# Splitting one product of three blocks into seven inner products, in a pooling mixer kernel with float32 accuracy

## The chip, the cores and the metric

The kernel runs on one core of a Trainium2 chip. The metric is the device time of one execution in microseconds (us). Engines are named as the profile names them: PE is TensorE (matmuls), PEld its weight loads, DVE is VectorE, ACT is ScalarE, POOL is GpSimd, SP is SyncE, which here issues DMAs.

## The reference

Of the hybrid trunk only the pooling layer runs, since the depth is 1. With x of 4096 rows and 1024 columns, all in float32:

```python
normed = rms_norm(h, norm_w[i])                 # row-wise, 1024 columns
u, gate = jnp.split(normed @ in_w, 2, axis=-1)  # in_w: 1024 x 2048
ug = u.reshape(b, s, 4, 256)
pooled = stack(trailing_mean(ug[:, :, g], w) for g, w in enumerate((2, 4, 8, 16))) - ug
mixed = jnp.einsum('bsgc,gcd->bsgd', pooled, group_w) + group_b
y = mixed.reshape(b, s, 1024) * scale * jax.nn.silu(gate)
h = h + y @ out_w                               # out_w: 1024 x 1024
out = rms_norm(h, final_norm_w)
```

Nearly all the arithmetic is in two matrix products, `normed @ in_w` and `y @ out_w`.

## The kernel before, in words

**Exactness.** Every float32 operand is held as a pair of tiles: a rounded copy (`copy`, L165, on ACT) and the rest (`sub`, L159, on DVE). `split` makes the pair. One product of two such operands is three matmuls (`mm3`, L603): high by high, high by low, low by high.

**Seven products in place of eight.** Each large product is one level of the Strassen-Winograd scheme: P1 to P7, where sums and differences of quarter matrices are formed on DVE beforehand and results are accumulated in PSUM banks. A step is one of these products. There are 28 steps of the first input phase ("a": half of the input projection, four blocks of 1024 rows), 28 of the second ("b": the other half, same rows, normalized operands read back from DRAM), and 56 of the output phase ("o", eight blocks of 512 rows).

**A step of phase b** (`product_in`) multiplies two operand tiles of 128 x 1024 pairs (`t[0]`, `t[1]`) by weight tiles `w[i]`. Weights of 128 x 128 are loaded and 512 columns stream by, 48 matmuls in all. The order of steps is P1, P2, P7, P6, P5, P4, P3. P1, P2, P7 and P4 use banks 0 to 3 ("x" and "v"), P6, P5 and P3 banks 4 to 7 ("y"). P1 goes bank by bank and its sums are copied to the y banks as seeds; the others go through `t[0]` for all four banks, then `t[1]`. After each step `evict_in` copies or adds the banks into SBUF: after P2 four ACT copies with Silu, after P7 four ACT copies to `ev["22"]`, after P5 and P4 DVE additions.

**Buffers.** Four operand tiles `ops` (op0 to op3) are used in turn, two by a step, so the pair for the next step is made while the present one multiplies. Eleven tiles `st` and eight wider tiles `vt` hold everything else: raw operands loaded ahead, evicted results, weights being prepared, window sums. `take` hands out the one that has been free longest, `give` returns it. Who waits for whom through these tiles is decided by this order.

**The order of work.** The program is written step by step; a scheduler places the instructions on each engine's queue, and each engine then takes its queue in that order. In each turn of the step loop: loads for up to three steps ahead are issued (`load`), the operand pair for the next step is made (`split_step`), sums for the step after that are formed (`form`), window sums that have come due are computed (`pool`: scans L755, L801, L806, then a store to `yd`), the step itself runs (`run`). In blocks 1 and 2 of phase b the weights of the output phase are prepared after P5 (`make_wo`: four loads of `out_w`, scaled on ACT at L246, combined on DVE, stored to `wod`). In block 3 each step is followed by `load_w`: the output phase's weights for the same product are loaded from `wod` and split into the same `w` tile that the step has just used. DMAs of these kinds all go through SP's queue.

**Where the same scheme is already used.** In the output phase from block 2 on, P2 is split into seven inner products (`product_inner`, L701), with 256 columns in each matmul.

Of the kernel before, what the change touches and what calls it, by code (L numbers as in the profile page):

```python
# [10 lines left out]
F32 = mybir.dt.float32  # L11
# [4 lines left out]
P = 128  # L16
D = 1024
# [47 lines left out]
def kernel(  # L65
# [59 lines left out]
    st.renew = renew  # L125
    vt = Slots(
        [mem.tile([P, 2 * (HIST + H)], F32, tag=f"vt{i}", name=f"vt{i}") for i in range(NV)]
    )
# [368 lines left out]


    xs = [{} for _ in range(NB)]
    turn = [0]  # L500
# [6 lines left out]
    first_saves = []  # L507

    def split_halves(us, saved=None):
        ts = []  # L510
        for h, u in enumerate(us):
            t = next_op("p (s a b) -> p s a b", s=2, a=2)
            split(t, u)
# [33 lines left out]
    def form_in(q, b, i):  # L547

        s = xs[b]
        if i in (P1, P2):  # L550
            if q == 0:
                for u in s["11" if i == P1 else "12"]:
                    normalize(b, 0, u)
        elif i == P7:
            if q == 0:
                for h in range(2):
                    normalize(b, 1, s["21"][h])
                    sub(s["21"][h], s["11"][h], s["21"][h])
        elif i == P6:
            s["2"] = [take(pool=early if (q, b) == (0, 0) else None) for _ in range(2)]  # L560
            for h in range(2):
                if q == 0:
                    normalize(b, 1, s["22"][h])
                sub(s["2"][h], s["22"][h], s["21"][h])
            for u in s.pop("21"):
                give(u)
            if q == 0:
                give(rstd.pop(b))
        elif i == P5:
            for h in range(2):  # L570
                add(s["11"][h], s["2"][h], s["11"][h])
            if (q, b) != (0, 0):
                for u in s.pop("2"):
                    give(u)

    def split_in(q, b, i):
        s = xs[b]
        key = {P1: "11", P2: "12", P6: "2", P7: "21", P5: "11", P4: "22", P3: "12"}[i]
# [11 lines left out]
    stores = []  # L590

    def form_s4(b):
        for u, s2 in zip(xs[b]["12"], xs[b]["2"]):
# [49 lines left out]
    def form_inner(stage):  # L643

        pattern, sizes = "p (n k s a) -> p n k s a", dict(n=2, k=2, s=2)
        if stage == 0:
            us = inner_w.pop("raw")
            b11, b12 = (quarter(us[0], j) for j in range(2))
            b21, b22 = (quarter(us[1], j) for j in range(2))
            raw = inner_w["sums"] = [take(pattern, **sizes) for _ in range(2)]  # L650
            (t3, t2), (t1, t4) = ([r[:, n] for n in range(2)] for r in raw)
            sub(t3, b22, b12)
            add(t2, t3, b11)
            sub(t1, b22, t2)
# [5 lines left out]
        hi, lo = (kept.pop().rearrange(pattern, **sizes) for _ in range(2))  # L660
# [483 lines left out]
    def run(n, between=None, behind=None, seeds=4):  # L1144
# [3 lines left out]
            product_out(i, split_up.pop(n), sets, n == len(steps) - 1)  # L1148
            evict_o(b, i, sets)
        else:  # L1150
            product_in(i, split_up.pop(n), sets, i == P1, between, behind)
            evict_in(b, 0 if kind == "a" else 1, i, sets, seeds)

    pending = []

# [204 lines left out]

    scales, summed = {}, []
    stages = (P6, P5, P4)
    stages = (P6, P5, P4)

    for n in range(2, len(steps)):
        kind, b, i = steps[n]
# [121 lines left out]
```

## Time and profile before

| what | value |
|---|---|
| median of 3 runs | 910.34 us (910.04 to 911.31) |
| the profiled execution | 910.49 us, span 908.7 us |
| PE busy | 900.7 us, 99% of the span, 4320 matmuls |
| DVE busy | 715.5 us, 79% |
| ACT busy | 485.9 us, 53% |
| chain that ended last | PE 95% of it |

The span is the time between the first and the last instruction; the execution's own time has 1.8 us around it. A group row reads: line, engine, operation, output<-input, shapes, count, then busy time in all and the mean of one in ns, then idle time of the engine just before them and what ended it. A timeline row reads: start and length in us, engine, line, operation, and in brackets the idle time before it with its releaser. A windows row has the busy time of each engine in one stretch, then the granted PE clock and the share of the DMA engines.

### The profile page before, as it was taken

The page shows a single profiled execution, that of the slowest core. Times are in us where ns is not written, and L with a number is a line of the kernel's source. Part 1 is how long each engine was busy: PE and PEld are TensorE (multiplying, and loading weights), DVE is VectorE, ACT ScalarE, POOL GpSimd, SP SyncE. Part 2 cuts the span into 40 slices and gives each one's busy share as a digit, 9 for nine tenths or more (in the row PEclk, how much of TensorE's full clock was granted, in tenths as well). Part 3 has the DMA queues.
Part 4 walks back from the last instruction along what each step waited for, and adds up shares of the span by engine and source line. Part 5 has one row for each costly group of instructions (what it writes and reads, how often), then busy time and mean ns, then how long its engine had stood idle before and what let it go on. Part 6 is the DMA issues. An engine that isn't in the chain of part 4 may idle for free.

```text
span 908.7 us, 11590 instructions
## 1 busy us (share of the span) xinstructions
PE 900.7 (99%) x4320; PEld 790.1 (87%) x4320; DVE 715.5 (79%) x843; ACT 485.9 (53%) x735; POOL 84.6 (9%) x166
## 2 busy tenths in 40 slices
PE   9999999999999999999999999999999999999997
PEld 7888888888888888888888888888888898988886
DVE  3889995985995997685786599599759768868686
ACT  7869547447446555355345445645545535445444
POOL 0020100100110000000000000001122113212200
PEclk9999999999999999999999999999999999999999
DMA  9987776577575454134616715618585675675732
GB/s 343 401 300 230 268 241 240 190 267 245 218 271 193 162 207 140 47 140 138 255 72 217 267 70 174 200 54 225 179 234 160 169 205 162 163 220 156 180 139 94
DMA packets 70841, 178.10 MB, mean 196 GB/s; under 512 B 6528, under 2 KB 24320, under 8 KB 70784
## 3 DMA queue, kind: packets, MB, share of 16 engines
q1 hardware_dynamic: 58160, 144.82, 46.0%
q0 software_dynamic: 11904, 31.48, 13.3%
q10 hardware_dynamic: 720, 1.06, 0.3%
q8 instruction: 34, 0.56, 0.3%
q14 instruction: 23, 0.19, 0.1%
HBM read 116.50 MB, written 60.83 MB: 195 GB/s over the span
## 4 chain that ended last, share of the span: by engine, by line
PE 95%; DVE 2%; DMA 1%; ACT 1%; issue 0%; DVEq 0%; ACTq 0%; SPq 0%
PE bank L603 89%; PE bank L701 3%; PE bank L406 3%; DMA st<-wvd 1%; DMA t3d<-st 0%; DMA early<-in_group_w 0%; DVE vt L1067 0%; DVE st L159 0%; ACT st L974 0%; ACT st L446 0%; DVE vt L162 0%; PE bank L472 0%; DVE op L159 0%; DVE vt L1026 0%; DVE st L156 0%
## 5 line engine op out<-in xcount | busy, mean ns | idle before, releaser
L603 PE MATMUL bank<-op,w 128*128 128x512 f32 x2688 | 581.2, 379 | 0.2 <-ACT st L165 0.2
L603 PEld LDWEIGHTS bank<-op,w 128*128 128x128 f32 x2688 | 507.8, 189 | 72.9 <-ACT st L165 0.6
L603 PE MATMUL bank<-w,op 128*128 128x512 f32 (+1 forms) x1212 | 262.2, 377 | 0.0
L603 PEld LDWEIGHTS bank<-w,op 128*128 128x128 f32 x1212 | 226.0, 189 | 31.0
L159 DVE TENSOR_TENSOR op<-st,op 128x1024 fp32r<-128x1024 f32 x129 | 156.5, 1220 | 76.4 <-ACT op L165 76.0
L165 ACT ACTIVATE op<-st 128x1024 fp32r<-128x1024 f32 x129 | 134.7, 1052 | 123.3 <-PE bank L603 82.6
L165 ACT ACTIVATE vt<-bank 128x512 f32<-128x512 f32 x105 | 61.4, 593 | 44.7 <-PE bank L603 44.2
L159 DVE TENSOR_TENSOR op<-vt,op 128x1024 fp32r<-128x1024 f32 x43 | 52.4, 1220 | 20.8 <-ACT op L165 20.6
L165 ACT ACTIVATE op<-vt 128x1024 fp32r<-128x1024 f32 x43 | 45.0, 1052 | 28.9 <-PE bank L603 24.9
L165 ACT ACTIVATE st<-bank 128x512 f32<-128x512 f32 x67 | 39.0, 592 | 38.0 <-PE bank L603 26.1
L884 POOL DMA_DIRECT2D st<-in_x x19 | 16.9, 894 | 387.7 <-DVE op L159 354.1
L159 DVE TENSOR_TENSOR st<-st,st 128x1024 f32<-128x1024 f32 (+1 forms) x43 | 46.7, 1108 | 3.2 <-ACT st L943 1.3
L165 ACT ACTIVATE bank<-bank 128x512 f32<-128x512 f32 x48 | 27.9, 581 | 35.6 <-PE bank L603 35.4
L755 DVE TENSOR_TENSOR_SCAN vt<-vt,window 128x1040 f32<-128x1040 f32 x16 | 38.1, 2379 | 2.8 <-ACT vt L165 2.7
L159 DVE TENSOR_TENSOR w<-st,w 128x1024 fp32r<-128x1024 f32 x25 | 30.2, 1220 | 11.7 <-ACT w L165 11.7
L165 ACT ACTIVATE w<-st 128x1024 fp32r<-128x1024 f32 x25 | 26.0, 1052 | 16.3 <-PE bank L603 10.8
L806 DVE SCALAR_TENSOR_TENSOR st<-vt,colt,st 128x512 f32<-128x512 f32 x46 | 32.4, 746 | 1.7 <-ACT st L165 1.6
L165 ACT ACTIVATE st<-st 128x1024 f32<-128x1024 f32 x16 | 16.9, 1058 | 29.9 <-DVE st L156 29.7
L801 DVE SCALAR_TENSOR_TENSOR vt<-vt,vt 128x1024 f32<-128x1024 f32 x24 | 29.3, 1221 | 0.3
L947 DVE SCALAR_TENSOR_TENSOR vt<-vt,ors,st 128x1024 f32<-128x1024 f32 x18 | 22.5, 1282 | 8.0 <-POOL ors L225 8.0
L162 DVE TENSOR_TENSOR st<-st,vt 128x1024 f32<-128x1024 f32 x22 | 26.1, 1216 | 2.1 <-DMA vt<-rd 2.1
L1067 DVE TENSOR_TENSOR st<-bank,st 128x512 f32<-128x512 f32 x23 | 15.8, 689 | 13.8 <-PE bank L603 13.7
(136 smaller groups left out, 661.6 us busy)
## 6 DMA issues: line engine op xcount, KB each, us to landing
st<-in_xt SPq DMA_DIRECT2D x28, 512.0 KB, 5.9
sd<-st POOLq DMA_DIRECT2D x28, 512.0 KB, 4.3
st<-sd SPq DMA_DIRECT2D x24, 512.0 KB, 4.4
yd<-st SPq DMA_DIRECT2D x23, 512.0 KB, 2.6
st<-in_x SPq DMA_DIRECT2D x20, 512.0 KB, 6.3
st<-yd SPq DMA_DIRECT2D x20, 512.0 KB, 4.7
out<-vt SPq DMA_DIRECT2D x18, 512.0 KB, 4.5
st<-wod SPq DMA_DIRECT2D x15, 512.0 KB, 3.4
```

The lines of the kernel that those rows point to most:

```text
L159: return nc.vector.tensor_tensor(out=dst, in0=a, in1=b, op=ALU.subtract)
L162: nc.vector.tensor_tensor(out=dst, in0=a, in1=b, op=ALU.mult)
L165: return nc.scalar.activation(dst, src, func)
L406: latest[0] = nc.tensor.matmul(ps, a[:, kk, 2 * j + t, :], maps, start=t + m == 0, stop=t == 1 and m == len(pairs) - 1,).ins
L603: latest[0] = nc.tensor.matmul(ps, a, b, start=start and n == 0, stop=stop and n == 2, skip_group_check=True).ins
L701: latest[0] = nc.tensor.matmul(ps, x1, x2, start=i in (P1, P7) and k + n == 0, stop=k == 1 and n == 2, skip_group_check=True,).ins
L755: nc.vector.tensor_tensor_scan(out=sums_[:, HIST:], data0=flat[:, HIST:], data1=flat[:, HIST - win : 2 * end - win], initial=first_sum, op ...
L801: nc.vector.scalar_tensor_tensor(out=s[:, :, at : at + H], in0=s[:, :, at : at + H], scalar=1.0 / win, in1=v[:, :, HIST:], op0=ALU.mult, o ...
L806: nc.vector.scalar_tensor_tensor(out=sg[:, j], in0=s[:, j, at : at + H], scalar=bias_c[2 * grp + j], in1=sg[:, j], op0=ALU.add, op1=ALU.mult,)
L884: nc.gpsimd.dma_start(out=hs[b][half, j][:, n], in_=x[row_of(b, half, j), n * H : (n + 1) * H], accum_op=ALU.add,)
L947: nc.vector.scalar_tensor_tensor(out=us[j], in0=us[j], scalar=rs[:, j : j + 1], in1=fw[0], op0=ALU.mult, op1=ALU.mult,)
L1067: partial["added"] = nc.vector.tensor_tensor(out=dst, in0=src, in1=dst, op=ALU.add).ins
```

## The change

In blocks 1, 2 and 3 of phase b, the step P7 is itself computed by seven inner products of half the size in each direction (p1 to p7 below, to tell them from the outer ones). Block 0 is left as it is.

Each inner product multiplies a 256 x 256 part of the weights into one of four "cells" of the banks (two half banks each; cell 0 and 2 in banks 0 and 1, cell 1 and 3 in banks 2 and 3), in 12 matmuls of 256 columns. No further bank is used: p5 goes to cell 3 and is copied out to an SBUF tile `held`, p1 to cell 1, and running sums are moved from cell to cell by ACT copies (`move`). At the end two DVE additions put `held` back into banks 2 and 3.

P7's operands now fill all four `ops` tiles: `front` (for p5, p3) and the first raw operand (p1) are made while P2 runs, `back` (p7, p6) when P2's first half has let its tile go (`second`), the second raw operand (p2, p4) after P2's evictions (`third`). The pair for the next step, P6, is no longer made one step ahead: it is made inside P7, its first half after p2 and its second after p4 has been written down (`middle`, `end`), in the tiles that p1 and p6/p7 let go. The list `ops` is rotated to the order in which they come free.

The weights of the inner products are formed once, in steps P6, P5, P4 and P3 of block 0 (`form_seven`): t3 is loaded again from `t3d`, four differences are formed, one pair goes into the quarter of `w[P7]` that is no longer needed, three pairs into `st` tiles that stay taken until block 3's P7 is over.

```diff
     def renew(t):
         i = next(i for i, u in enumerate(sts) if u is t)
-        return mem.tile([P, D], F32R, tag=f"st{i}", name=f"inner{i}")
+        return mem.tile([P, 2, H], F32R, tag=f"st{i}", name=f"inner{i}")
...
     def next_op(pattern, **sizes):
-        t = ops[turn[0] % 4]
-        turn[0] += 1
+        t = ops.pop(0)
+        ops.append(t)
         return t.rearrange(pattern, **sizes)
...
+    def inner_in(q, b, i):
+
+        return q == 1 and b > 0 and i == P7
...
+    def split_seven(s):
+
+        us = s["21"]
...
+        front, back = (take("p (n k s a) -> p n k s a", n=2, k=2, s=2) for _ in range(2))
+        sub(back[:, 0], a11, a21)
+        sub(back[:, 1], a22, back[:, 0])
+        add(front[:, 0], back[:, 1], a11)
+        sub(front[:, 1], a12, back[:, 1])
...
+        sums(front, (P5, P3))
+        plain_op(0, {P1: 0})
+
+        def second():
+            sums(back, (P7, P6))
+
+        def third():
+            plain_op(1, {P2: 0, P4: 1})
+            for u in s.pop("21"):
+                give(u)
+            ops[:] = [ops[n] for n in (1, 2, 0, 3)]
...
+    def form_seven(stage):
+
+        if stage == 0:
+            seven["raw"] = [take() for _ in range(2)]
+            for h, u in enumerate(seven["raw"]):
+                nc.sync.dma_start(out=u, in_=t3d[h])
+            return
...
+    def product_seven(t, v, middle, end):
+
+        def cell(n, c):
+            return v[2 * (n % 2) + c][:, n // 2 * 256 : (n // 2 + 1) * 256]
+
+        def into(i, n):
+            for c in range(2):
+                cs = slice(c * P, (c + 1) * P)
+                for k in range(2):
+                    a = [o[:, k, cs] for o in seven_w[i]]
+                    b = [o[k] for o in t[i]]
+                    for m, (x1, x2) in enumerate(((a[0], b[0]), (a[0], b[1]), (a[1], b[0]))):
+                        latest[0] = nc.tensor.matmul(
+                            cell(n, c).rearrange("p (a s) -> p a s", s=2), x1, x2,
+                            start=i == P5 and k + m == 0, stop=k == 1 and m == 2,
+                            skip_group_check=True,
+                        ).ins
+
+        def move(dst, src):
+            for c in range(2):
+                copy(cell(dst, c), cell(src, c))
+
+        held = take()
+        into(P5, 3)
+        into(P1, 1)
+        for c in range(2):
+            copy(held[:, c, 0:256], cell(3, c))
+        move(0, 1)
+        into(P6, 1)
+        into(P2, 0)
+        move(2, 1)
+        middle()
+        into(P7, 2)
+        into(P3, 1)
+        move(3, 2)
+        into(P4, 2)
+        end()
+        for c in range(2):
+            bank = v[2 + c].rearrange("p (j b) -> p j b", j=2)
+            add(bank, bank, held[:, c, 0:256].unsqueeze(1).to_broadcast([P, 2, 256]))
+        give(held)
...
+            q = 0 if kind == "a" else 1
+            if inner_in(q, b, i):
+                us, parts = xs[b]["2"], []
+                at["split"] += 1
+
+                def next_half():
+                    parts.append(split_half(us[len(parts)]))
+
+                product_seven(split_up.pop(n), sets["v"], next_half, next_half)
+                if b == NB - 1:
+                    give_kept(*places_in)
+                split_up[n + 1] = parts
+            else:
+                product_in(i, split_up.pop(n), sets, i == P1, between, behind)
+            if "second" in seven:
+                seven.pop("second")()
+            evict_in(b, q, i, sets, seeds)
+            if "third" in seven:
+                seven.pop("third")()
+            if inner_in(q, b, i):
+                form_s4(b)
+                for u in xs[b].pop("2"):
+                    give(u)
...
     def split_reach(kind, b, i):
+        if kind == "b" and b > 0 and i == P6:
+            return 0
         return 2 if kind == "o" and (b, i) != (0, P1) else 1
...
+        if kind == "b" and b == 0 and i in forming_seven:
+            with tc.issue_after(latest_split[0]), tc.issue_after(latest_copy[0]):
+                form_seven(forming_seven.index(i))
```

More of the change, by code (lines that the diff above doesn't have):

```diff
@@ L122, in renew, with give_kept, next_kept @@
         i = next(i for i, u in enumerate(sts) if u is t)
-        return mem.tile([P, D], F32R, tag=f"st{i}", name=f"inner{i}")
+        return mem.tile([P, 2, H], F32R, tag=f"st{i}", name=f"inner{i}")
     st.renew = renew
+    def give_kept(*places):
+        for i in places:
+            sts[i] = mem.tile([P, D], F32, tag=f"st{i}", name=f"st{i}")
+            Slots.clock += 1
+            st.free.append((Slots.clock, sts[i]))
+    def next_kept():
+        return next(i for i, u in enumerate(sts) if u is st.free[0][1])
     vt = Slots(
@@ new lines @@
+    seven_w, kept_in, places_in = {}, [], []
+    def form_seven(stage):
[4 more added lines that the diff above has]
+            return
+        us = seven["raw"]
+        if stage == 1:
+            t1, t3 = (us[0][:, :, j * 256 : (j + 1) * 256] for j in range(2))
+            t4, t2 = (us[1][:, :, j * 256 : (j + 1) * 256] for j in range(2))
+            sub(t1, t3, t1)
+            sub(t3, t2, t3)
+            sub(t2, t2, t1)
+            sub(t4, t4, t2)
+            seven["sums"] = {P5: t1, P6: t2, P7: t3, P4: t4}
+            for p, (h, j) in {P1: (0, 0), P2: (1, 0), P3: (1, 1)}.items():
+                seven_w[p] = [w[P7][h][:, v, :, j * 256 : (j + 1) * 256] for v in range(2)]
+            for _ in range(3):
+                places_in.append(next_kept())
+                kept_in.append(st.keep())
+            return
+        for p in ((P5, P6), (P7, P4))[stage - 2]:
+            if p == P5:
+                home = [w[P7][0][:, v, :, 256:512] for v in range(2)]
+            else:
+                t = kept_in.pop().rearrange("p v (k c) -> p v k c", k=2)
+                home = [t[:, v] for v in range(2)]
+            latest_copy[0] = copy(home[0], seven["sums"][p]).ins
+            latest_split[0] = sub(home[1], seven["sums"][p], home[0].bitcast(F32)).ins
+            seven_w[p] = home
+        if stage == 3:
+            for u in seven.pop("raw"):
+                give(u)
@@ L659, in form_inner @@
         r = inner_w["sums"][stage - 1]
[L660 removed]
+        hi, lo = (
+            kept.pop().rearrange("p x (y s a) -> p x y s a", y=2, s=2) for _ in range(2)
+        )
         copy(hi, r)
```

44 lines of the change are left out of this document (35 added, 9 removed).

## The prediction

> **What bounds the kernel now.** First the page's busy times, then PE's own waits, then windows cut at step boundaries:
>
> ```profile
> span 908.7 us, 11590 instructions
> PE 900.7 (99%) x4320; PEld 790.1 (87%) x4320; DVE 715.5 (79%) x843; ACT 485.9 (53%) x735; POOL 84.6 (9%) x166
> ...
> PE bank L603 <- ACT st L165: 0.2, 1, 0.2
> ...
> 397.30:469.80 72.50, 72.50 (x338) 63.48 (x337) 53.15 (x53) 34.66 (x52) 0.00 (x0) 1.00 0.46 167
> 542.30:552.70 10.40, 10.40 (x50) 9.11 (x49) 9.67 (x12) 5.22 (x10) 0.00 (x0) 1.00 0.29 110
> 552.70:563.00 10.30, 10.30 (x50) 9.01 (x49) 10.11 (x9) 5.68 (x9) 0.00 (x0) 1.00 0.66 218
> 563.00:573.40 10.40, 10.40 (x50) 9.11 (x49) 8.13 (x7) 7.16 (x10) 0.00 (x0) 1.00 0.40 115
> ```
>
> PE is the bound: in the large products it waited 0.2 us in all. Block 1 takes 72.50 us for seven steps, so 10.36 each. Whatever shortens PE's work shortens the run, and every new PE wait lengthens it. The last three rows are P1, P2 and P7 of block 3: DVE is busy 9.67, 10.11 and 8.13 of some 10.3 us there, so around this P7 DVE has almost nothing free.
>
> **The gain.** From the chain of waits and the groups:
>
> ```profile
> 702.93 3.35 PE bank L701 x30
> 706.28 2.59 PE bank L603 x12
> ...
> L603 PE MATMUL bank<-op,w 128*128 128x512 f32 x2688 | 581.2, 379 | 0.2 <-ACT st L165 0.2
> L701 PE MATMUL bank<-inner,op 128*128 128x256 f32 x144 | 20.0, 275 | 0.0
> L701 PEld LDWEIGHTS bank<-inner,op 128*128 128x128 f32 x144 | 18.9, 191 | 0.7
> ```
>
> A 256-column matmul costs 3.35/30 = 0.112 us, a 512-column one 2.59/12 = 0.216. P7 goes from 48 x 0.216 = 10.36 to 84 x 0.112 = 9.38: 0.98 us a block, 2.94 in three. This is the whole gain.
>
> The Trainium skill (TensorE: Matmul & The Clock Gate, Part 3, "What overlaps and what doesn't") has it that a weight load overlaps running matmuls only where they use other rows of the array. By that each of the 84 would add its own load, and the change would lose far more than it saves. The row of 30 in 3.35 us, each with a 128x128 load, does not bear it out.
>
> **Hand-offs inside P7** (blocks 1 to 3). Sizes:
>
> ```profile
> 418.07 0.60 ACT L165 ACTIVATE vt<-bank 128x512 f32<-128x512 f32 x1 [0.70 <-PE bank L603]
> 418.56 1.99 ACT L165 ACTIVATE op<-st 128x1024 fp32r<-128x1024 f32 x2
> ...
> L974 ACT ACTIVATE st<-vt 128x512 f32<-128x512 f32 x5 | 3.2, 633 | 9.1 <-DVE vt L711 7.0 <-DVE vt L1067 2.0
> L974 ACT ACTIVATE st<-vt 128x256 f32<-128x256 f32 x2 | 0.8, 409 | 0.0
> ...
> 220.27 0.61 ACT st L165
> 220.88 0.04 issue
> 220.92 482.01 PE bank L603 x2232
> ...
> 220.92 0.92 PE L603 MATMUL bank<-op,w 128*128 128x512 f32 x3 [0.22 <-ACT st L165]
> ```
>
> 418.07 is P2's fourth eviction in block 1. Its last matmul runs 0.38, the next enters after 0.22, and the copy follows the drain by 0.04, so P7 entered at 417.87. A copy thus starts 0.20 us after its bank's last matmul has been followed. The next ACT instruction enters 0.49 later. A 256-column copy is 0.60 - (0.633 - 0.409) = 0.37 long and holds ACT 0.27. PE resumes 0.04 after a copy, and the three matmuls then take 0.92 where 2 x 0.216 + 0.38 = 0.81 is normal: 0.15 in all.
>
> With t from P7's start and 0.67 for six matmuls (one column of an inner product): p5's second column waits for the fourth eviction, 0.20 + 0.60 + 0.15 = 0.95 against 0.67: lost 0.28. p1 ends at 2.96. Only when its first column is done (2.29, seen at 2.49) can ACT copy p5 to `held` (0.27) and p1 to cell 0 (0.37): 3.13, p6 at 3.28: lost 0.32. p2 runs to 5.97, the move that p7 needs ends at 5.87, p7 at 6.02: lost 0.05. p7 and p3 run to 8.70, but on ACT the split of P6's second half (1.0 us, behind p7's end at 7.56) stands before the next move: that one ends at 8.88, p4 at 9.03: lost 0.33. Sum 0.98: P7 takes 10.36 again, +0.0 a block. Bounds from these rows: every hand-off covered, -0.98; twice the losses, +1.0. I take the walk. The two DVE additions at the end are free, under P6 in the other banks.
>
> **Formation of weights, block 0**: two 512 KB loads on SP, four ACT copies of 0.6, eight DVE instructions of 0.68 (5.4 us). Cover is the rest of DVE's queue in P6 to P3, and window sums slide by as much. By the queues of the changed kernel the first casualty would be a seed copy of block 1's P1 standing on ACT behind a "tails" copy that waits for a scan; it comes out level with PE. 0 taken, at most 1.0.
>
> **Block 2.** Added there and in block 3: two splits (ACT 1.0, DVE 1.2 each), four sums (0.62 each), and two tiles from `take`, beside three `st` tiles that stay taken.
>
> ```profile
> 465.77 1.23 DVE L159 TENSOR_TENSOR op<-st,op 128x1024 fp32r<-128x1024 f32 x1 [0.79 <-ACT op L165]
> 412.71 1.34 ACT L246 ACTIVATE st<-st,colt 128x512 f32<-128x512 f32 x2 [3.46 <-DMA st<-in_out_w]
> ...
> L755 DVE TENSOR_TENSOR_SCAN vt<-vt,window 128x1040 f32<-128x1040 f32 x16 | 38.1, 2379 | 2.8 <-ACT vt L165 2.7
> L806 DVE SCALAR_TENSOR_TENSOR st<-vt,colt,st 128x512 f32<-128x512 f32 x46 | 32.4, 746 | 1.7 <-ACT st L165 1.6
> ...
> L156 DVE TENSOR_TENSOR st<-bank,st 128x512 f32<-128x512 f32 x32 | 20.8, 682 | 0.0
> ...
> st<-in_out_w SPq DMA_DIRECT2D x6, 512.0 KB, 4.0
> st<-wod SPq DMA_DIRECT2D x15, 512.0 KB, 3.4
> ...
> yd<-vt SPq DMA_DIRECT2D x9, 512.0 KB, 3.5
> ```
>
> A load of `out_w` goes into the tile of P7's raw operand, behind the subtraction that reads it last. Its scaling (two on ACT, 1.24 us) stands in ACT's queue before the evictions of P2's banks 1 to 3. From the split of P2's first operand (465.77 before, 468.0 when one scan with its follow-up has slid behind, 3.5 us into a stretch with some idle time) to the end of that subtraction DVE has two scans (2.38), four sums (0.62 pitch), four L806 (0.67 pitch), seven full-size ones (1.14 pitch) and 0.3 of small ones, 18.2 us: 486.2. Load 3.4 to 3.5 (the low end of such loads, whose median here is 4.0), scaling 489.8 to 491.0, banks 1 and 2 to 492.1, PE at 492.3; P7 is due at 490.4. Lost 1.9 in place of 0.28, so +1.6 for the block. Bounds: with 465.77 as start only the 0.28 (+0.0); with a load of 4.5, +2.7.
>
> **Block 3.**
>
> ```profile
> 540.43 2.38 DVE L755 TENSOR_TENSOR_SCAN vt<-vt,window 128x1040 f32<-128x1040 f32 x1 [0.91 <-ACT vt L165]
> 546.58 2.38 DVE L755 TENSOR_TENSOR_SCAN vt<-vt,window 128x1040 f32<-128x1040 f32 x1
> 552.33 1.23 DVE L159 TENSOR_TENSOR w<-st,w 128x1024 fp32r<-128x1024 f32 x1 [0.66 <-ACT w L165]
> 553.47 1.22 DVE L159 TENSOR_TENSOR op<-st,op 128x1024 fp32r<-128x1024 f32 x1
> ...
> 551.24 1.06 ACT L165 ACTIVATE w<-st 128x1024 fp32r<-128x1024 f32 x1 [0.50 <-PE bank L603]
> 559.43 1.06 ACT L165 ACTIVATE w<-st 128x1024 fp32r<-128x1024 f32 x1 [3.79 <-DMA st<-wod]
> 560.40 1.07 ACT L165 ACTIVATE vt<-bank 128x512 f32<-128x512 f32 x2
> 561.81 0.60 ACT L165 ACTIVATE st<-bank 128x512 f32<-128x512 f32 x1 [0.35 <-PE bank L603]
> ```
>
> Before, the two scans of block 2's last group run under P1 (540, 546). In the changed queues the first one writes the tile that held `front`, free only when `front` is split at P1's end, so DVE idles under P1 and the scans follow after 552.33. From there its queue is, by 1.14 pitch: w1 552.33, front 553.47, scan 554.7, w1 557.0, first raw operand, two subtractions (the first frees the tile that w2's load needs: 560.5), L801, `back` 562.7, two L806 to 565.3, scan to 567.6, w2, L801, second raw operand 569.8 to 571.0.
>
> ACT's queue: w2 (load 560.6 + 3.4 = 564.0), evictions of banks 0 and 1 (these write tiles that the two L806 read), second raw operand, two small copies behind the second scan (567.6), and only then the evictions of banks 2 and 3, which p5 needs. The tile of the first is on its way to `yd` until 565.35 + 3.5 = 568.85. So p5 enters at 568.87 + 0.60 + 0.15 = 569.6 where 562.9 was due: lost 6.7. p5 and p1 end at 572.3. Behind the first copy to `held` stands the second half of w2 on ACT: its load follows DVE's 571.0, lands at 574.45; split (0.95), `held`, move: PE resumes p6 at 576.2, lost another 3.9. Then 0.05, and 0.4 before p4. Sum 11.1 - 0.98 = **+10.1**. Before, the third eviction ended at 562.4, and PE needed that bank only 2.6 us into P7: cover of 3 us. Bounds: if only one of the two long waits is met, +6; if loads take 4.5 each and the store as well, +12.5.
>
> In the other queues: w7, w6 and later loads slip on SP behind the same two tiles, but the output phase needs them from 615 us on.
>
> **Sum.** 0.0 (block 0) + 0.0 + 1.6 + 10.1 = +11.7 on the profiled execution's 910.49 (span 908.7; the median of the runs, 910.34, is 0.15 below): **922.2 us**. Own range 916.5 (+6 in block 3 alone) to 926.7 (+1.0, +2.7 and +12.5).
>
> **Rivals.**
> - *Faster.* DVE and ACT reach P2's third eviction in time in block 3 (the second scan over by 559) and most hand-offs are covered: -2.94 + 1 = 908.5. For it: DVE is 79% busy over the run. Against: 10.11 of 10.3 us in P2 of block 3.
> - *No change.* The queues keep up, the hand-offs cost what the columns save: 910.6. For it: +0.0 in block 1.
> - *Weight loads not covered.* 0.19 us each on top of 0.112: 84 x 0.30 = 25 us in place of 10.36, three times: 955. Against: the L701 rows.
> - *The clock drops in the 6.7 us gap.* The rows below: PE's last matmul ends at 902.1, and a mean clock of 0.83 over the last 3.7 us is half speed from about 907.4, 5.3 us later. Half speed for p5 and p1 hides under w2's load; if it lasts some 5.6 us beyond, +2.8: 925. The Trainium skill (TensorE: Matmul & The Clock Gate, Part 1, "What's actually happening") gives an idle window of about 3.4 us; the trace's end agrees that a gap of this size is enough.
> - *Knock-on.* Later steps of block 3 or the first output blocks wait for operands too: 928 and up. Against: by the queues, nothing PE needs is late once P7 is over.
>
> ```profile
> 898.82 3.27 PE L603 MATMUL bank<-w,op 128*128 128x512 f32 x26
> 905.00:908.70 3.70, 0.00 (x0) 0.00 (x0) 0.32 (x1) 0.15 (x1) 0.00 (x0) 0.83 0.44 166
> ```
>
> **Chances.** Forecast 0.62, clock 0.10, knock-on 0.08, no change 0.09, faster 0.08, weight loads 0.03. A difference of 0.2% (1.8 us) is about what a measurement of this kernel can tell. Faster 0.08, same 0.09, slower 0.83. Range 912.5 to 928.5: from where slower begins, through the forecast's own range, to the clock case on top of its middle and the mildest knock-on. It leaves out faster, unchanged and the weight loads.
>
> **What would show it.** Right: PE waits of some 6 and 4 us in block 3's P7, released by ACT copies of the line of `copy`; scans of the last group after P1 instead of under it; 0.3 us waits before p5's second column, p6 and p4 in block 1; 256-column matmuls at 0.112. Wrong: block 3's evictions of banks 2 and 3 near 562; PE waits under 1 us there; or new waits outside P7.

## The result, and the profile after

The changed kernel takes 924.21 us (median; 923.57 to 925.47), the kernel before 910.19 us in the same comparison (909.97 to 911.31): ratio 1.0153, 95% interval 1.0136 to 1.0171. The forecast was 922.2 us. The profiled execution has a span of 922.9 us against 908.7. The page, then PE's own waits in the large products:

```profile
span 922.9 us, 11895 instructions
PE 904.6 (98%) x4428; PEld 795.6 (86%) x4428; DVE 736.1 (80%) x875; ACT 498.6 (54%) x769; POOL 85.1 (9%) x166
...
PE bank L708 <- ACT vt L175: 7.4, 2, 5.5
PE bank L708 <- ACT bank L175: 2.0, 1, 2.0
```

Where PE waited 0.2 us before, it now waits 9.4 us, in three places, all at matmuls of the new product (L708) and all released by ACT copies (L175). To see where the 14.2 us arose I compare the start of the same matmul in both traces, counted through the records (36 more in each of three blocks, e4's filling matmuls left out), and take the increase from one step boundary to the next. The same table serves the experiments. All values are us:

| stretch | after | e1 | e2 | e3 | e4 | e5 | e6 | e7 | e8 | e9 | e10 |
|---|---|---|---|---|---|---|---|---|---|---|---|
| start to block 1 | -0.16 | -0.95 | 0.02 | 0.82 | -0.40 | -0.55 | -0.50 | 1.60 | -0.24 | 1.75 | 0.64 |
| block 1: P1, P2 | 0.30 | 0.80 | 0.25 | 0.00 | 0.00 | 0.10 | 0.08 | 0.00 | 0.34 | 0.00 | 0.61 |
| block 1: P7 | 0.11 | 0.00 | 0.12 | 0.12 | 0.12 | 0.11 | 0.12 | -0.41 | -0.41 | -0.39 | -0.55 |
| block 2: to P7's entry | 2.15 | 2.07 | 2.25 | 2.12 | 2.20 | 0.00 | 2.20 | 0.00 | 0.00 | 0.00 | 0.00 |
| block 2: P7 | -0.07 | 0.00 | -0.07 | 1.35 | -0.07 | 0.11 | -0.07 | 1.68 | -0.40 | -0.39 | -0.55 |
| block 3: P1, P2 | 0.00 | 0.00 | 1.27 | 0.00 | 0.00 | 0.00 | 1.44 | 0.00 | 0.00 | 0.00 | 0.00 |
| block 3: P7's entry | 5.62 | 0.25 | 2.89 | 5.62 | 5.62 | 5.61 | 0.00 | 2.69 | 0.00 | 0.00 | 0.00 |
| block 3: P7 | 5.58 | 2.63 | 1.45 | 1.67 | 0.01 | 5.55 | 0.16 | 3.40 | 0.61 | -0.39 | -0.44 |
| rest of block 3, output phase | 0.28 | 4.30 | 0.25 | 0.26 | 0.27 | 0.34 | 0.26 | 0.25 | 0.25 | 0.25 | 0.32 |
| tail | 0.34 | 0.36 | 0.35 | 0.33 | 0.34 | 0.34 | 0.33 | 0.34 | 0.34 | 0.34 | 0.35 |
| span | 922.9 | 918.2 | 917.5 | 921.0 | 916.8 | 920.3 | 912.7 | 918.3 | 909.2 | 909.9 | 909.1 |

Block 3 costs 11.2 of the 14.2 us, block 2 costs 2.1, block 1 0.4. The first row holds PE's wait for the first loads and a wait near 220 us that stands behind a load of `wvd`; both differ from run to run. Now the places. In block 1, PE and ACT around P7 in the timeline of after:

```profile
418.01 3.13 PE L708 MATMUL bank<-op,w 128*128 128x256 f32 x24
421.23 0.94 PE L708 MATMUL bank<-op,inner 128*128 128x256 f32 x6
...
427.04 1.60 PE L708 MATMUL bank<-op,inner 128*128 128x256 f32 x12
428.49 2.75 PE L749 MATMUL bank<-op,w 128*128 128x512 f32 x12
...
408.08 0.23 ACT L175 ACTIVATE vt<-tails 128x32 f32<-128x32 f32 x1 [7.71 <-DVE vt L903]
408.21 0.58 ACT L175 ACTIVATE bank<-bank 128x512 f32<-128x512 f32 x1
```

P7 enters at 418.01 and leaves at 428.49: 10.47 us. Between matmuls that follow each other by 0.112 the records show four stretched steps: before p5's second column, before p6, p7 and p4, of 0.29, 0.34, 0.10 and 0.34 with the slower refill behind each: nearly all of the 1.09 by which P7 exceeds 9.38. The last two rows are P2's 0.3 us: a seed copy stands behind a copy of tails that waits for a scan.

In block 2, ACT and PE:

```profile
490.45 1.33 ACT L256 ACTIVATE vt<-vt,colt 128x512 f32<-128x512 f32 x2 [2.47 <-DMA vt<-in_out_w]
491.69 1.55 ACT L175 ACTIVATE vt<-bank 128x512 f32<-128x512 f32 x3
...
492.80 2.95 PE L708 MATMUL bank<-op,w 128*128 128x256 f32 x24 [1.99 <-ACT vt L175]
```

The scaling of `out_w` waits for its load, and the three evictions wait behind it. In block 3, PE, DVE's scans, ACT with the store to `yd` that SP issues and the time to its landing, and then the granted clock in windows cut where it changes (columns as before: PE, PEld, DVE, ACT, POOL busy, clock, DMA share, GB/s):

```profile
570.87 5.49 PE L708 MATMUL bank<-op,w 128*128 128x256 f32 x24 [5.45 <-ACT vt L175]
578.37 1.78 PE L708 MATMUL bank<-op,inner 128*128 128x256 f32 x12 [2.02 <-ACT bank L175]
579.95 2.77 PE L708 MATMUL bank<-op,w 128*128 128x256 f32 x12
...
557.07 2.38 DVE L903 TENSOR_TENSOR_SCAN vt<-vt,window 128x1040 f32<-128x1040 f32 x1
567.49 2.38 DVE L903 TENSOR_TENSOR_SCAN vt<-vt,window 128x1040 f32<-128x1040 f32 x1
...
566.30 1.06 ACT L175 ACTIVATE w<-st 128x1024 fp32r<-128x1024 f32 x1 [4.97 <-DMA st<-wod]
567.27 1.06 ACT L175 ACTIVATE vt<-bank 128x512 f32<-128x512 f32 x2
568.22 1.06 ACT L175 ACTIVATE op<-st 128x1024 fp32r<-128x1024 f32 x1
569.90 0.35 ACT L175 ACTIVATE vt<-tails 128x32 f32<-128x32 f32 x2 [0.62 <-DVE vt L903]
570.22 1.09 ACT L175 ACTIVATE vt<-bank 128x512 f32<-128x512 f32 x2
...
567.60 0.32 SPq L958 DMA_DIRECT2D yd<-vt  x1
DMA to landing us min/median/max: 2.6/2.6/2.6
...
576.72 1.06 ACT L175 ACTIVATE w<-st 128x1024 fp32r<-128x1024 f32 x1 [1.22 <-DMA st<-wod]
...
565.30:569.40 4.10, 0.12 (x1) 0.00 (x0) 4.10 (x4) 2.97 (x4) 0.00 (x0) 1.00 0.33 135
569.40:576.20 6.80, 5.33 (x24) 5.19 (x24) 6.80 (x8) 1.79 (x5) 0.00 (x0) 0.50 0.31 100
576.20:579.70 3.50, 1.48 (x12) 1.33 (x12) 2.69 (x5) 2.84 (x5) 0.00 (x0) 0.99 0.34 139
579.70:583.10 3.40, 3.40 (x18) 3.40 (x17) 2.74 (x3) 0.65 (x3) 0.00 (x0) 0.50 0.52 154
583.10:587.50 4.40, 4.40 (x39) 4.32 (x38) 3.28 (x4) 4.18 (x7) 0.00 (x0) 1.00 0.22 73
```

Both scans run after P1, the first in P2 and the second while PE already waits. ACT's first two evictions stand behind w2's load and split (566.30). The last two stand behind the copies of tails that the second scan releases (569.90), and the third eviction also waits for the store to `yd`: it lands 2.6 us after its issue, at 570.19 by the trace's semaphore record, and that eviction starts at 570.22. Then the half clock: 6.8 us of it from 569.4 on, once more from 579.7 for 3.4 us, behind the second wait.

### The profile page after: what moved, and what is told of

Read it like the earlier page. It is cut to its first block, busy times and chain, and to the rows that moved or that the text cites. A ratio compares the mean times of both kernels' runs of the same rounds, so it can differ in the third digit from the quotient of the medians.

```text
span 922.9 us, 11895 instructions
## 1 busy us (share of the span) xinstructions
PE 904.6 (98%) x4428; PEld 795.6 (86%) x4428; DVE 736.1 (80%) x875; ACT 498.6 (54%) x769; POOL 85.1 (9%) x166
## 4 chain that ended last, share of the span: by engine, by line
PE 87%; DVE 7%; DMA 3%; issue 1%; ACT 1%; SPq 0%; DVEq 0%; ACTq 0%
PE bank L749 80%; PE bank L849 3%; PE bank L708 3%; DVE op L169 1%; DVE vt L903 1%; DMA early<-in_wut 1%; DMA st<-in_x 1%; PE bank L416 1%; DVE vt L949 1%; DVE vt L169 0%; DMA early<-in_group_w 0%; DVE w L169 0%; DMA st<-wod 0%; DVE vt L954 0%; DMA vt<-in_out_w 0%
## 5 line engine op out<-in xcount | busy, mean ns | idle before, releaser
L749 PE MATMUL bank<-op,w 128*128 128x512 f32 x2544 | 550.8, 379 | 0.0
L749 PEld LDWEIGHTS bank<-op,w 128*128 128x128 f32 x2544 | 480.3, 189 | 68.7 <-ACT bank L175 0.8
L175 ACT ACTIVATE op<-st 128x1024 fp32r<-128x1024 f32 x133 | 139.3, 1053 | 114.6 <-PE bank L749 68.3
L175 ACT ACTIVATE vt<-bank 128x512 f32<-128x512 f32 (+1 forms) x116 | 66.2, 591 | 44.2 <-PE bank L749 42.5
L175 ACT ACTIVATE op<-vt 128x1024 fp32r<-128x1024 f32 x45 | 47.2, 1054 | 28.8 <-PE bank L749 22.2
L175 ACT ACTIVATE bank<-bank 128x512 f32<-128x512 f32 (+1 forms) x66 | 34.5, 524 | 36.6 <-PE bank L749 31.3
L175 ACT ACTIVATE st<-bank 128x512 f32<-128x512 f32 (+1 forms) x62 | 34.9, 577 | 34.6 <-PE bank L749 18.5
L169 DVE TENSOR_TENSOR st<-st,st 128x1024 f32<-128x1024 f32 (+2 forms) x37 | 38.8, 1060 | 1.9 <-ACT st L1091 1.2
L169 DVE TENSOR_TENSOR w<-st,w 128x1024 fp32r<-128x1024 f32 (+1 forms) x24 | 28.3, 1195 | 6.2 <-ACT w L175 6.2
L175 ACT ACTIVATE w<-st 128x1024 fp32r<-128x1024 f32 (+1 forms) x24 | 24.5, 1032 | 12.9 <-DMA st<-wod 7.5
L708 PE MATMUL bank<-op,w 128*128 128x256 f32 x144 | 22.2, 314 | 7.5 <-ACT vt L175 7.4
L708 PEld LDWEIGHTS bank<-op,w 128*128 128x128 f32 x144 | 20.8, 227 | 8.5 <-ACT vt L175 8.5
L175 ACT ACTIVATE vt<-tails 128x32 f32<-128x32 f32 x28 | 6.3, 228 | 40.5 <-DVE vt L903 19.3
L175 ACT ACTIVATE st<-st 128x1024 f32<-128x1024 f32 x14 | 14.8, 1059 | 24.1 <-DVE st L166 24.0
```

The source lines that it names most:

```text
L169: return nc.vector.tensor_tensor(out=dst, in0=a, in1=b, op=ALU.subtract)
L175: return nc.scalar.activation(dst, src, func)
L708: latest[0] = nc.tensor.matmul(cell(n, c).rearrange("p (a s) -> p a s", s=2), x1, x2, start=i == P5 and k + m == 0, stop=k == 1 and m == 2 ...
L749: latest[0] = nc.tensor.matmul(ps, a, b, start=start and n == 0, stop=stop and n == 2, skip_group_check=True).ins
```

## The experiments

Each diff is against the changed kernel. The times of e1 to e7 are of one execution with 1.8 to 3.2 us around its span, so there I compare the spans and the table.

**e1: block 3 alone.**

```diff
-        return q == 1 and b > 0 and i == P7
+        return q == 1 and b in (3,) and i == P7
...
-        if kind == "b" and b > 0 and i == P6:
+        if kind == "b" and b in (3,) and i == P6:
```

(P7 of blocks 1 and 2 here multiplies by a quarter of `w[P7]` that `form_seven` has already overwritten, so those values are not the reference's; the instructions are the same.)

> P7 as seven inner products in block 3 alone; blocks 1 and 2 as before, so the eleven st and eight vt tiles are handed out in another order and the two scans of block 2's last group stand ahead of P1's end in DVE's queue again. Theory A (the long wait before block 3's P7 comes from those scans, which in the changed kernel could only start once the tile of front was free): PE enters P7 of block 3 less than 1 us late; the wait for the second half of w2 before p6 stays, 3 to 4 us; in all 913.5 us (912.5 to 915). Rival B (the added work itself, two splits and four sums, overfills P2 of block 3, wherever the scans stand): a wait of 4 to 6 us before p5 stays, 919 us or more.

919.95 us, span 918.2. DVE's scans of the last group and PE at P7:

```profile
542.87 2.38 DVE L903 TENSOR_TENSOR_SCAN vt<-vt,window 128x1040 f32<-128x1040 f32 x1
549.02 2.38 DVE L903 TENSOR_TENSOR_SCAN vt<-vt,window 128x1040 f32<-128x1040 f32 x1
...
565.08 3.12 PE L708 MATMUL bank<-op,w 128*128 128x256 f32 x24
```

Block 3 comes out as theory A has it: the scans are back under P1, PE enters P7 0.25 late, and the block costs 0.25 + 2.63 = 2.9 in place of 11.2. It does not single out the scans, since w2's split also runs earlier here, at 559.32 in place of 566.30. The total was missed by 6 us: the other order of the tiles brings new waits outside. In block 2's P2 it is 2.07, behind a scaling of `out_w` that waits for its load. In the output phase it is 4.3: a wait of 2.05 before a matmul of its split P2 (859.11), and half clock from 860.2 to 863.6 behind it. Since the change of tile order moved waits in other phases too, the edits that follow keep the three blocks.

**e2: scans early.**

```diff
-            wait = 1 + int(b == 0) if kind == "a" else 2 if b < NB - 1 else 5
+            wait = 1 + int(b == 0) if kind == "a" else 1 if b == NB - 2 else 2 if b < NB - 1 else 5
```

> All three blocks as in the changed kernel, but the window sums of block 2's last group are due one step earlier, in P1 of block 3, so they get their tiles before front does. Nothing else is edited. Theory A: both scans run under P1; the evictions of P2's third and fourth bank end by about 566 (P7 due at 565.25 with the 2.35 us that blocks 1 and 2 cost), the wait of 5.6 us before p5 falls below 1 us, and w2's second half stands behind the first moves on ACT, so the wait before p6 goes too: 913.5 us (912.5 to 914.5). Rival B (too much work in P2 of block 3): waits of 4 us or more stay around P7, 919 us or more.

920.68 us, span 917.5. Block 3 costs 1.27 + 2.89 + 1.45 = 5.6 in place of 11.2, so half of it came back where theory A said nearly all. ACT and PE:

```profile
568.04 1.06 ACT L175 ACTIVATE w<-st 128x1024 fp32r<-128x1024 f32 x1 [3.08 <-DMA st<-wod]
569.00 1.06 ACT L175 ACTIVATE vt<-bank 128x512 f32<-128x512 f32 x2
...
569.63 4.57 PE L708 MATMUL bank<-op,w 128*128 128x256 f32 x24 [2.72 <-ACT vt L175]
```

The scans are out of the way, and what now stands ahead of evictions 3 and 4 is w2's load and split. In the changed kernel that was over at 567.3, hidden behind the scans. The wait inside P2 (1.0, a seed copy behind `front`'s split) is new. The wait before p6 is gone, as expected; the 1.45 in P7 comes from half clock (570.6 to 574.0), which the theory did not have.

**e3: w2 late.**

```diff
-                load_w(wod, i)
+                if i == P7:
+                    with tc.issue_after(evicted[0]):
+                        load_w(wod, P2)
+                        load_w(wod, P7)
+                elif i != P2:
+                    load_w(wod, i)
```

> All three blocks as in the changed kernel, but in block 3 the output phase's weights w2 are loaded and split only after P7's evictions instead of after P2's. Theory A: the wait before p5 stays, since evictions 3 and 4 wait for scans and the store behind them: PE enters P7 5 to 6 us late; the wait before p6 goes. PE then runs P7 at the half clock that the trace of the changed kernel shows from 569.4 to 576.25, no longer hidden under the load of w2, so P7 takes some 12.7 us: 920.5 us (919.5 to 921.5). Rival C (the load and split of w2 on ACT, ahead of the evictions, are what makes p5 late): p5 less than 1.5 us late, 914 us.

922.94 us, span 921.0. Theory A: PE enters P7 5.62 late as before, and P7 loses 1.67 in place of 5.58, so the wait before p6 was w2's second half. The total lies above its range (919.5 to 921.5). That the span fell by 1.9 only has other reasons: the start (1.0 later than in the changed kernel) and 1.4 more in P7 of block 2, where the clock halved for 3.4 us after the same wait that had cost no clock in the changed kernel (see the last section).

**e4: w2 late, PE kept busy.** Beside e3's edit:

```diff
+    zero = const.tile([P, P], mybir.dt.bfloat16, name="zero")
+    nc.gpsimd.memset(zero, 0.0)
+    ones = nc.const_aps.tensor(1.0, [P, H], mybir.dt.bfloat16)
+    def keep_warm(count):
+        with tc.issue_after(latest[0]):
+            for j in range(count):
+                latest[0] = nc.tensor.matmul(banks[4 + j % 4], zero, ones, start=False, stop=False,
+                    skip_group_check=True).ins
...
+        keep_warm(warm[0])          # 25 in block 3
         into(P5, 3)
```

> As the kernel with w2 late, and ahead of p5 in block 3 PE runs 25 matmuls of 512 columns with weights of zero into the y banks (they add 0; some 5.4 us, as long as the wait). The queues of ACT, DVE and SP are the same instructions in the same order. If the half clock after the wait is what idle PE time brings on: granted clock 1.0 throughout, P7 2.7 us shorter than in the kernel with w2 late, 917.8 us (917.2 to 918.4). Rival D (the clock drops for another reason, or its cost is hidden behind the moves anyway): no shorter by more than 0.5 us, 920 us or more.

918.57 us, span 916.8. The same stretch of e4 (first the filling matmuls, then P7) and of e3 (the wait, then p5 and p1, then the rest) in windows:

```profile
564.90:570.40 5.50, 5.43 (x26) 2.27 (x24) 5.50 (x5) 3.02 (x7) 0.00 (x0) 1.00 0.24 95
570.40:580.70 10.30, 10.06 (x84) 9.64 (x85) 10.06 (x13) 6.15 (x13) 0.00 (x0) 1.00 0.64 204
```

```profile
567.50:572.90 5.40, 0.00 (x0) 0.00 (x0) 5.40 (x5) 2.96 (x7) 0.00 (x0) 0.70 0.24 97
572.90:576.20 3.30, 3.25 (x15) 3.26 (x16) 3.30 (x5) 0.48 (x1) 0.00 (x0) 0.50 0.53 159
576.20:579.60 3.40, 3.26 (x27) 3.07 (x27) 3.40 (x4) 2.25 (x5) 0.00 (x0) 0.96 0.37 154
```

P7 of block 3 is 1.66 shorter (0.01 against 1.67) with the queues of ACT, DVE and SP unchanged: the half clock comes from PE's idling, and it is worth 1.7 here. The 2.7 expected came from the changed kernel, where the half clock ends 5.4 us after p5 starts; in e3 it ends 3.5 us after. The total, just above its range, also holds e4's own start and a block 2 without e3's half clock, so the 1.7 are read from the table.

**e5: out_w's scaling late.**

```diff
-                make_wo(b - 1)
+                with tc.issue_after(evicted[0]):
+                    make_wo(b - 1)
```

> All three blocks as in the changed kernel, but the scaling of out_w on ACT is queued behind the evictions of P6 in both blocks that prepare it. Theory: the 2.15 us that PE waits before block 2's P7 come from that scaling, which stands ahead of evictions 2 to 4 of P2 and waits for its load; with it gone PE enters P7 of block 2 less than 0.4 us late, the other blocks keep their losses (block 3: 11.2 us), and the run takes 922.1 us (921.5 to 923; a half clock after the gaps in another phase may add up to 1.5). Rival (DVE's backlog in block 2, or the subtraction that the load waits for, makes the evictions late): PE still waits over 1.5 us there, 924 us.

923.07 us, span 920.3. The wait before block 2's P7 is gone, 0.00 in place of 2.15, and block 3 keeps its 11.2. The cause is shown; the single time lies just above the expected 921.5 to 923, while the span is 2.6 below the changed kernel's.

**e6: e2's and e3's edits together.**

> The two edits for block 3 together: window sums of block 2's last group one step earlier, and w2 loaded and split after P7's evictions. Each alone left 4.2 and 5.6 us of wait before p5. Theory (two causes, each enough to hold evictions 3 and 4: the scans with their store, and the load and split of w2 on ACT): with both gone PE enters P7 of block 3 less than 0.6 us late, P7 takes about 10.4 us, and only the 1.0 us wait inside P2 (front's split ahead of a seed copy) stays: 1.3 to 1.8 us for the block in place of 11.2, in all 914.6 us (913.8 to 915.6). Rival (a third cause: DVE is simply full in P1 and P2): 3 us or more of wait before p5 or p6, 917 us or more.

914.5 us, span 912.7. PE's waits:

```profile
PE bank L708 <- ACT vt L175: 2.0, 1, 2.0
PE bank L749 <- ACT bank L175: 1.2, 1, 1.2
```

The 2.0 is block 2's, the 1.2 the one inside P2 of block 3. P7 of block 3 starts on time and loses 0.16: block 3 costs 1.6 in place of 11.2. So two causes held evictions 3 and 4. With the scans alone PE came 5.62 late to P7 (e3), with w2 alone 1.27 + 2.89 = 4.16 (e2), with neither 1.44, all of it from P2. DVE is not too full.

**e7: inside P7.**

```diff
-            return v[2 * (n % 2) + c][:, n // 2 * 256 : (n // 2 + 1) * 256]
+            return v[2 - 2 * (n % 2) + c][:, n // 2 * 256 : (n // 2 + 1) * 256]
...
-        move(3, 2)
+        moved = move(3, 2)
         into(P4, 2)
-        end()
+        with tc.issue_after(moved):
+            end()
...
-            bank = v[2 + c].rearrange("p (j b) -> p j b", j=2)
+            bank = v[c].rearrange("p (j b) -> p j b", j=2)
```

(Here and in e8 the evictions were not exchanged with the banks, so the two halves of P7's output columns change places.)

> The changed kernel with two edits inside P7: p5 and p1 go to the banks that are evicted first (cells 1 and 3 in banks 0 and 1), and the split of P6's second half is queued on ACT behind the last move. By the hand-offs as walked (0.28 before p5's second column, 0.33 before p4), P7 of block 1 takes 9.85 us in place of 10.47, block 2's 9.7 in place of 10.3, block 3 gains about 0.3 (its first copies wait for something else): 922.8 us, of which the start of the run may move 0.6 either way. Rival (PE cannot refill between so short groups, and the loss is not ACT's copies): P7 of block 1 stays above 10.3.

920.82 us, span 918.3: 2 us below the expectation, since block 3 came out 4.8 shorter than expected and the start 1.8 longer. P7 of block 1 takes 9.95 in place of 10.47: the two hand-offs give back 0.52 of the 0.61 that the walk gave them. In block 2 the wait for `out_w` moves to p5's second column (1.7), since its first bank is now evicted ahead of the scaling. Block 3 fell to 6.1 with another order of ACT's queue, and some 1.6 of that is half clock again (573.8 to 577.2); what the new order released is open.

**e8: all edits** (e5, e6, e7, and `front`'s split queued behind P1's last seed copy).

> All edits together: scans early, w2 late, scaling of out_w late, the two edits inside P7, and front's split queued behind P1's last seed copy in every block. If the causes are those named and nothing new takes their place, each block keeps the shorter P7 (about 9.85 us in place of 10.36, so -0.5), with 0.3 for P2 of block 1, 0.3 in block 3's P2 and 0.6 in the output phase and the tail, as in all kernels so far: 910.0 us, within 0.1% of the kernel before (909.0 to 911.2). If one cause was only moved: 912 us or more.

911.12 us against 910.02: ratio 1.0013 (1.0004 to 1.0023). Blocks 1 and 2 gain 0.41 and 0.40 in P7 and no long wait is left but one: in block 3, 0.7 before p2's second matmul.

```profile
PE bank L708 <- DVE op L169: 0.7, 1, 0.7
```

The second raw operand's DVE half is late there, behind two subtractions for S4. So 13 of the 14 us come back with the causes named, and the changed P7 still gains nothing.

**e9: p5 and p1 in different banks.** As e8 without e7's exchange of banks:

```diff
-        into(P5, 3)
+        into(P5, 2)
         into(P1, 1)
-            copy(held[:, c, 0:256], cell(3, c))
-        move(0, 1)
-        into(P6, 1)
+            copy(held[:, c, 0:256], cell(2, c))
+        for c in range(2):
+            copy(held[:, c, 256:512], cell(1, c))
         into(P2, 0)
+        into(P6, 1)
...
+            add(cell(0, c), cell(0, c), held[:, c, 256:512])
```

(`start` is set for p1 too, and `form_s4` is queued behind the last split. In this kernel cell 3, which ACT alone writes, is overwritten by P4 instead of added to (see e10 and the last section), so half of each block's rows lack P7's part.)

> As the kernel with all edits, but the exchange of banks inside P7 is replaced by another order, by which the output stays in its place: p5 goes to cell 2 (banks 0 and 1), p1 to cell 1 (banks 2 and 3), both are copied to halves of held, then p2 runs into cell 0 before p6, and two more DVE additions of 256 columns put p1 back into cell 0 at the end. S4's subtractions are queued on DVE behind the split of P6's second half. If the loss inside P7 is PE waiting for copies that read the bank it must write next, no such wait is left over 0.2 us: P7 takes 9.4 to 9.6 us in each block, -0.8 to -0.95 against the 10.36 of the kernel before. With 0.3 in P2 of block 1, 0.25 in the output phase and 0.34 in the tail, as in the other kernels, the run takes 908.5 us (907.8 to 909.5), 0.1 to 0.25% below the kernel before. Rival (the short groups cost PE by themselves, or the added DVE work holds p2 or p4 back): P7 stays at 9.9 or more, 910 us or more.

910.25 us against 910.29: ratio 0.9998 (0.9989 to 1.0007). P7 takes 9.97, not 9.4 to 9.6. The hand-offs are gone but for one of 0.37, at p2's second matmul, and 0.1 before each of p7 and p4. DVE's row beside it:

```profile
421.39 1.23 DVE L169 TENSOR_TENSOR op<-st,op 128x1024 fp32r<-128x1024 f32 x1 [3.28 <-ACT op L175]
```

p2 comes 1.34 us earlier than before, and its second matmul, due at 422.41, needs this half; it is there at 422.62, and the matmul starts at 422.67. The rival's second half, DVE work that holds p2 back, is what happened.

**e10: the same, mended.**

```diff
+                        if i == P1 and k + m == 0:
+                            out = v[2 * (n % 2) + c].rearrange("p (j a s) -> p j a s", j=2, s=2)
+                            x2 = x2.unsqueeze(1).to_broadcast([P, 2, P, 2])
...
+                if c == 3 and "third" in seven:
+                    seven.pop("third")()
+                with tc.issue_after(latest_copy[0]) if c == 3 and inner_in(q, b, P7) else nullcontext():
```

> As the kernel with p5 and p1 in different banks, with two edits. p1's first matmul of each column is 512 columns wide, so that it writes cell 3 as well as cell 1; that costs 2 x 0.104 us, and the whole computation is then the reference's. The second raw operand's split is queued on ACT ahead of P2's fourth eviction, so that its DVE half is over before p2. If the 0.37 us that P7 lost before p2 in the last kernel was that DVE half, P7 takes 9.6 to 9.8 us in every block (9.38 + 0.21 + small refills), 0.55 to 0.75 less than in the kernel before; three times that, less 0.25 in the output phase, 0.34 in the tail and up to 0.34 in P2 of block 1: 909.1 us (908.5 to 909.8). Rival (eviction 4, now later, holds p1's second column): P7 at 9.9 or more, 910 us or more.

909.58 us against 910.41: ratio 0.9992 (0.9983 to 1.0001). PE at P7 of block 1:

```profile
419.11 4.39 PE L712 MATMUL bank<-op,w 128*128 128x256 f32 x36
423.34 2.96 PE L712 MATMUL bank<-op,inner 128*128 128x256 f32 x24
426.13 1.50 PE L712 MATMUL bank<-op,w 128*128 128x256 f32 x12
427.48 1.60 PE L712 MATMUL bank<-op,inner 128*128 128x256 f32 x12
428.92 1.25 PE L757 MATMUL bank<-op,w 128*128 128x512 f32 x5
```

No waits inside: 9.81 us from entry to P6, at the upper end of what was expected (9.92 in block 3). Three times 0.5 are gained, and 0.6 in P2 of block 1, 0.3 in the rest of block 3 and the output phase, and 0.35 in the tail take most of it. It is the best version of the seven products found, 14.6 us below the changed kernel, and not to be told from the kernel before.

## Why the prediction was right, and where its terms were off

The direction, the places and nearly the sum were right: 922.2 forecast, 924.2 measured. By its steps:

- *The gain.* Right: the new matmuls follow each other by 0.112 us with a 128 x 128 load each, and 84 of them take 9.38. The rival of uncovered weight loads (955 us) fell. With it fell, for this kernel, the rule of the Trainium skill that spoke for it (TensorE: Matmul & The Clock Gate, Part 3, "What overlaps and what doesn't").
- *Hand-offs, 0.98.* Measured 1.09 in block 1, in the places named (0.29, 0.34, 0.10 and 0.34 for 0.28, 0.32, 0.05 and 0.33), and 0.9 in block 2. e7 takes 0.52 out of the first and the last.
- *Block 0, 0.* The formation itself cost nothing that the traces show; but the casualty named, a seed copy behind a copy of tails, came 0.3 late in block 1, not level.
- *Block 2, +1.6.* Mechanism right, shown by e5. Measured 2.08. The load was issued behind a subtraction that ended at 487.0 (row below), not 486.2, and the wait before P7 came to 2.15 in place of 1.9; and P7 itself then gained 0.07 in place of 0.28.

```profile
485.78 1.22 DVE L169 TENSOR_TENSOR st<-st,vt 128x1024 f32<-128x1024 f32 x1
```

- *Block 3, +10.1.* Measured 11.2, and the two waits are the two forecast: 6.7 and 3.9 by the walk, 5.6 and 2.0 in the trace, the second short because p5 and p1 ran at half clock before it. P1 ended 2.35 later than in the kernel before; with that the walk put the starts of the two scans at 557.05 and 567.65 (measured 557.07 and 567.49), p5's entry at 571.95 (570.87), p6 at 578.55 (578.37). The release of evictions 3 and 4 was right in kind and wrong in size. The third eviction did wait for the store to `yd`, but the store took 2.6 us (so also in e3 and e5) where the walk took 3.5, the median of nine such stores before, and the eviction started at 570.22 instead of 571.2. The copies of tails behind the second scan were done at the same time: the second ended at 570.25, and the trace shows such copies followed within 0.15 us of their start. Both go back to the scans. What the walk did not price is that w2's first half would hold the same evictions nearly as long by itself (e2).
- *The clock.* A rival at 0.10, and it happened, at about half the price that it named. As its sentence said, the first half clock hid under w2's load. The second spell (579.7 to 583.1) was not foreseen: it followed the second wait, and cost 15 matmuls 0.1 each, 1.5 us. By the Trainium skill (TensorE: Matmul & The Clock Gate, Part 1, "What's actually happening") a window of about 3.4 us decides; the spells of 6.83 and 3.41 us agree. The traces add that 2 us of idle time in such a window were enough (last section).
- *The sum.* 14.2 measured in the spans against 11.7. Of the 2.5 between, 1.5 are the second spell of half clock, 0.5 block 2, 0.4 block 1 and 0.6 the output phase with the tail; block 3 without that spell came out 0.4 shorter than the walk, and the start 0.2. The misses are small and mostly of one sign, so the sum is near by its large terms and not by their cancelling.
- *Left out.* 0.28 in the output phase and 0.34 in the tail, in nearly every kernel of the study, whatever its P7 looked like. The 0.25 that all of them share arise at one matmul of the first split P2 of the output phase, whose weight load waits for an operand's DVE half in the changed kernel (row below) and does not wait in the kernel before. The tail's 0.34 lie behind the issue of the last output store (905.18 of 908.7 before, 919.01 of 922.9 after), and their cause is open.

```profile
717.34 0.52 PEld L849 LDWEIGHTS bank<-w,op 128*128 128x128 f32 x4 [0.17 <-DVE op L169]
```

- *No change, faster.* Both need the evictions in time and covered hand-offs. e8 to e10 show that this has a price of its own, and that even then the 2.94 us shrink to 0.8 at most, within the measurement.

## What to carry to other kernels

When a step that engine queues used to cover is replaced by one that asks for its inputs earlier, price the cover, not the step: here 0.98 us of matmul time a block was bought by moving the need for two evictions from 2.6 us into the step to its start. Walk the in-order queues of the engines that feed the step, and for each late copy ask what stands second ahead of it, since the first cause can hide one of nearly the same size. Here most of the hand-offs between groups of a few matmuls went away once the next group wrote another bank than the one being copied and work that must follow was queued behind the copies: P7 of block 1 went from 10.47 to 9.81 us (e10).

## What the runs showed of the hardware

- A wait of two us can halve PE's clock or not. In the changed kernel PE was idle from 490.81 to 492.80 at no cost; in e3, after the same wait 0.7 us later (491.49 to 493.45), the clock was 0.5 from 494.58 to 497.99 and P7 took 1.4 us more. Spells that end inside a run last 3.41 us or twice that. In the changed kernel they start at 569.42, 579.66 and 920.99, the later two 3 and 103 steps of 3.413 after the first; in e3 two start at 494.58 and 569.67, 22 such steps apart. So time is cut in fixed pieces of 3.413 us, and counted back from the spells the pieces that hold the two waits, and the pieces behind them, are these (the changed kernel, then e3):

```profile
490.91:494.33 3.42, 1.53 (x13) 1.53 (x14) 0.83 (x3) 3.27 (x6) 0.00 (x0) 1.00 0.37 153
494.33:497.74 3.41, 3.33 (x30) 3.14 (x29) 3.41 (x4) 2.29 (x5) 0.00 (x0) 1.00 0.00 0
...
491.17:494.58 3.41, 1.45 (x12) 1.13 (x11) 1.13 (x2) 3.41 (x6) 0.00 (x0) 1.00 0.37 154
494.58:497.99 3.41, 3.41 (x19) 3.41 (x18) 3.13 (x3) 0.93 (x4) 0.00 (x0) 0.50 0.00 0
```

  In the changed kernel 0.1 us of the wait falls into the piece before, and 1.89 us of idle time left the clock alone; in e3 all 1.96 us fall into one piece. All twelve traces, cut in this way, fit, with idle time counted between the matmul records (whose ends are modelled): every piece with 2.02 us or more of idle time was followed by half clock, no piece at full clock with 1.89 or less was, and of two with 1.96 one was (e3) and one was not (the kernel before, 900.65 to 904.06). Where a wait of this length falls among the pieces thus decides its price, and the pieces lay differently in each trace. Why the limit lies there is not shown.
- The first matmul with `start` in a bank has an effect on the whole bank. In e9, p1's `start` in cell 1 made P4, which adds to what P7 leaves, overwrite cell 3, though ACT had written it in between; in e10, where p1's first matmul also writes cell 3, P4 adds again. The Trainium skill (PSUM — Partial Sum Buffer, "The four PSUM rules") says the same: the flag clears marks over a whole 2 KiB bank, and only matmuls set them again.
- A matmul group that resumes after a wait takes some 0.1 us more at its first step, in each stretched place of P7; the waits of 0.2 us are thus 0.3.
